# A Hyena loop that is skewed by half a channel group, its transforms copied out of PSUM by ScalarE

## The chip, the cores and the metric

The kernel runs on one core of one Trainium2 chip. TensorE (PE) multiplies matrices into PSUM, VectorE (DVE) and ScalarE (ACT) read PSUM and SBUF, GpSimd (POOL) does little here, SyncE (SP) issues the DMAs. Each engine takes its instructions in a fixed order and waits on semaphores for the others. The metric is the time of one execution in microseconds (us) on the device.

## What is computed

The reference is a two-layer diffusion backbone: an even layer with a recurrent part (RG-LRU) and a Hyena part, an odd layer with a convolution module, and after each a mixture of 16 experts. The change touches the Hyena part of the even layer alone:

```python
u = _dwconv1d(hy, p['conv_b_w'], p['conv_b_b'])     # three taps, 1536 channels
v, *gates = jnp.split(u, HYENA_ORDER + 1, axis=-1)  # 512 channels each
kf = _hyena_filters_fft(h.shape[1], p)
z = v
for o in range(HYENA_ORDER):                        # two orders, one after the other
    z = gates[o] * _fftconv(z, kf[:, o], p['filt_bias'][o])
return jnp.concatenate([y_a, z], axis=-1) @ p['w_out'], h_last
```

`_fftconv` is a convolution over 1024 tokens by a transform, a product with the filter's transform and the transform back.

## The kernel before

The 512 channels go in four groups of 128, and each group passes two convolutions, one for each order. I call the first convolution of group i J0(i) and the second J1(i); J1(i) starts from the gated result of J0(i). So there are eight jobs, and each is made of these steps:

- `short(ct)`: one projection on PE, 48 matmuls of 128x512 at lines 153 to 155 into one of two wide PSUM tiles `P`, then the three taps: ACT at line 767, DVE at lines 768 and 769. It gives a tile `y`: the input of J0, or a gate. There are twelve in the loop. The weights of a projection come in by `piece`, which splits them in two (ACT line 158, DVE line 159).
- `tok(y)`: eight transposes on PE (line 649) and two ACT copies (line 650) give `ut`, with tokens on the partitions.
- `hy_fwd`: 16 matmuls on PE (line 593) into four PSUM tiles `q`, and four ACT copies (line 596) of the second half of each.
- `hy_st1`: the radix-2 step, eight DVE operations of 128x256 (lines 603, 604), one operand in PSUM.
- `hy_mid`: two `fft8` (two operations of 128x512 and fourteen of 128x256 each, lines 565 to 582), and between them eight operations of 128x1024 (lines 614 to 621): the product with the filter's transform `K` and the first step back. All on DVE, all in SBUF.
- `hy_inv`: 16 matmuls on PE (line 632) into two PSUM tiles.
- `hy_gate`: two DVE products (line 640) of the PSUM tiles with the gate, written every eighth element into `zt`. For J0, `tok` follows, for J1 a store or the output projection.

`fill(n)` puts n pieces of other work between: four matmuls each (line 229) for the adaLN vectors, with a load of 1 MB each. `gate(ct)` is one of two more projections, for the RG-LRU output. The `K` of a job is loaded in `hy_fwd` into a ring of four buffers that the fills use too.

The program writes the jobs as J0(0), J1(0), J0(1), J1(1) and so on. A scheduler of the framework then sorts each engine's instructions, and that order is fixed when the program is built. The order of the twelve projections is 0, 4, 8, 1, 5, 9, 2, 6, 10, 3, 7, 11. Small PSUM tiles come from a pool of four, and all jobs use one pool of three SBUF tiles (tag `X`) for `pq` and `E`.

Of the kernel before, what the change touches and what calls it, by code (L numbers as in the profile page):

```python
# [9 lines left out]
F32 = mybir.dt.float32  # L10
# [5 lines left out]
OP = mybir.AluOpType  # L16
# [129 lines left out]
class Builder:  # L146
# [185 lines left out]
    def filt_mlp(self, p, f):  # L332
        nc, A = self.nc, self.A
        V = nc.vector
        zT = f.tile([66, 512], F32, name="zT")
# [42 lines left out]
    def filters(self, fk, other):  # L378
        nc, A = self.nc, self.A
        V = nc.vector  # L380
        c = math.sqrt(0.5)
# [201 lines left out]

    def hy_fwd(self, p, J):
        nc = self.nc
        J["K"] = K = self.wr.tile([128, 8, 2, 128], F32, name="w", tag="w")
        nc.sync.dma_start(K, self.kd[J["o"]][J["qd"]])
        J["q"] = []
        for a in range(4):
            q = self.ps.tile([128, 2, 2, 128], F32, name="q", tag="n")  # L590
            for j in range(2):
                for ri in range(2):
                    nc.tensor.matmul(q[:, j, ri], self.G[:, a + 4 * j, ri * 128:ri * 128 + 128], J["u"][:, a + 4 * j],  # L593
                                     start=True, stop=True)
            y4 = p.tile([128, 2, 128], F32, name="y4", tag="y4", bufs=2)
            nc.scalar.copy(y4, q[:, 1])
            J["q"].append((q, y4))

    def hy_st1(self, p, J):
        V = self.nc.vector  # L600
        J["pq"] = pq = p.tile([128, 8, 2, 128], F32, name="pq", tag="X", bufs=3)
        for a, (q, y4) in enumerate(J["q"]):
            V.tensor_tensor(pq[:, a], q[:, 0], y4, op=OP.add)
            V.tensor_tensor(pq[:, 4 + a], q[:, 0], y4, op=OP.subtract)

    def hy_mid(self, p, J):
        V = self.nc.vector
        pq, K = J["pq"], J["K"]
        E = p.tile([128, 8, 2, 128], F32, name="E", tag="X", bufs=3)
        sub = p.tile([128, 4, 2, 128], F32, name="sub", tag="sub", bufs=1)  # L610
        self.fft8(pq, E, -1, sub)
        Z = pq
        tmp = sub.rearrange("p a b c -> p (a b) c")
        V.tensor_tensor(Z[:, :, 0], E[:, :, 0], K[:, :, 0], op=OP.mult)
        V.tensor_tensor(tmp, E[:, :, 1], K[:, :, 1], op=OP.mult)
        V.tensor_tensor(Z[:, :, 0], Z[:, :, 0], tmp, op=OP.subtract)
        V.tensor_tensor(Z[:, :, 1], E[:, :, 0], K[:, :, 1], op=OP.mult)
        V.tensor_tensor(tmp, E[:, :, 1], K[:, :, 0], op=OP.mult)
        V.tensor_tensor(Z[:, :, 1], Z[:, :, 1], tmp, op=OP.add)
        V.tensor_tensor(E[:, 0:4], Z[:, 0:4], Z[:, 4:8], op=OP.add)  # L620
        V.tensor_tensor(E[:, 4:8], Z[:, 0:4], Z[:, 4:8], op=OP.subtract)
        self.fft8(E, Z, 1, sub)
        J["Z"] = Z
# [11 lines left out]
    def hy_gate(self, p, J):  # L635
        dst = p.tile([128, D], F32, name="zt", tag="zt", bufs=1)
        zv = dst.rearrange("q (p a) -> q a p", a=8)
        gv = J["gate"].rearrange("q (p a) -> q a p", a=8)
        for h, q in enumerate(J["r"]):
            self.nc.vector.tensor_tensor(zv[:, h * 4:h * 4 + 4], q, gv[:, h * 4:h * 4 + 4], op=OP.mult)  # L640
        return dst

    def to_tok(self, src, dst):
# [8 lines left out]
    def even_mixer(self, st, so):  # L652
        nc, tc, A = self.nc, self.tc, self.A
# [6 lines left out]
        with ExitStack() as s1, ExitStack() as sl:  # L660
# [66 lines left out]
            with ExitStack() as s2:  # L727
# [13 lines left out]
                w, P = xproj(0)  # L741
# [5 lines left out]
                for ct in range(4):  # L747
                    if ct:
                        w, P = xproj(ct)
# [7 lines left out]
            py = pool(s1, "py", "right")  # L757
            self.G = py.tile([128, 8, 256], F32, name="G2")
            gload = nc.sync.dma_start(self.G, A["G"].rearrange("p a r k -> p a (r k)"))
# [12 lines left out]
            def tok(y):  # L772
                ut = py.tile([128, 8, 128], F32, name="ut", tag="u", bufs=2)
                self.to_tok(y, ut)
                return ut

            pend = []

            def drain():
                J = pend.pop(0)  # L780
                self.hy_inv(py, J)
                z = self.hy_gate(py, J)
                if J["o"] == 0:
                    return tok(z)
                i = J["qd"]
                if i == 3:
                    return z
                nc.sync.dma_start(self.ycd[512 + i * 128:512 + (i + 1) * 128, :], z)

            for i in range(4):  # L790
                J0 = dict(o=0, qd=i, u=tok(short(i)))
                if i == 0:
                    with tc.issue_after(getattr(gload, "ins", gload)):
                        nc.sync.dma_start(self.IG, A["IG"])
                        self.fill(5)
                else:
                    self.fill(5)
                self.hy_fwd(py, J0)
                self.hy_st1(py, J0)
                if pend:  # L800
                    drain()
                self.hy_mid(py, J0)
                J0["gate"] = short(4 + i)
                self.fill(5)
                g1 = short(8 + i)
                pend.append(J0)
                J1 = dict(o=1, qd=i, u=drain(), gate=g1)
                self.hy_fwd(py, J1)
                self.hy_st1(py, J1)
                self.hy_mid(py, J1)  # L810
                pend.append(J1)
            for _ in range(len(self.ada_todo) + len(self.ada_have)):
                self.fill()
            for ct in (2, 3):
# [10 lines left out]
            with tc.tile_pool(name="pq0", bufs=1, reuse_waits="tile") as pq, \  # L825
                    tc.manual_schedule(engines={mybir.EngineType.PE, mybir.EngineType.DVE, mybir.EngineType.Activation}):
                y = self.y_load(pq, 0, 1)
                th = pq.tile([128, 7, 128], F32R, name="th")
                tl = pq.tile([128, 7, 128], F32R, name="tl")
                for q in range(2):  # L830
                    self.wide_hi(po, ws[q])
                    self.wide_lo(po, ws[q], q)
                self.mix_cast(0)
                self.bcast(self.sh2b, 0, 1)
                self.wide_hi(po, ws[2])
                z = drain()
                self.split(th, tl, y)
                self.split(self.zh, self.zl, z)
                self.wide_lo(po, ws[2], 2)
                self.wide_hi(po, ws[3])  # L840
                self.wide_lo(po, ws[3], 3)
                self.PP = [self.ps.tile([128, 512], F32, name="P", tag="w") for _ in range(2)]
                for k in range(8):
                    for n in range(2):
                        self.post_mm(self.PP[n], k, n, th[:, k] if k < 7 else self.zh[:, :128],
                                     tl[:, k] if k < 7 else self.zl[:, :128])
# [796 lines left out]
```

## Time and profile before

| what | value |
|---|---|
| median of three runs | 2298.85 us (2296.74 to 2299.62) |
| the profiled execution | 2297.13 us |
| its span, first to last instruction | 2295.1 us |
| PE busy over the span | 2123.7 us (93%) |
| DVE busy | 1819.8 us (79%) |
| ACT busy | 1201.7 us (52%) |
| Hyena stage, first radix-2 step to the last `fft8` | 281.45 to 547.74 us |

A PE that counts as busy is not always at its peak, since matmuls overlap in the record; what a row of equal matmuls takes from one start to the next tells its rate. The granted clock is a share of full speed: 1.0 is 2.4 GHz, 0.5 is 1.2 GHz. The rows on which the argument stands come below.

### The profile page before, as it was taken

Reading aid. Unit: us, or ns where it says so; the run is one execution under the profiler, and the core shown is the slowest. Engines: PE = TensorE matmul, PEld = TensorE weight load, DVE = VectorE, ACT = ScalarE, POOL = GpSimd, SP = SyncE. Lnnn points to the kernel's source line nnn. Section 1 sums busy time; section 2 is a strip of 40 time slices with the busy share of each in tenths; the row PEclk is TensorE's granted clock in tenths of the full one; section 3 lists DMA queues with packets and bytes.
Section 4 is the critical chain, followed back from the end, with each engine's and each line's share of the span. In section 5 each row is a group of like instructions: output and inputs, shape, how many; then the busy total and the mean of one; then the engine's idle time right before and its main releaser. Section 6 shows DMA issues by size and latency. Waiting matters only on the chain.

```text
span 2295.1 us, 29201 instructions
## 1 busy us (share of the span) xinstructions
PE 2123.7 (93%) x10882; PEld 1654.9 (72%) x10882; DVE 1819.8 (79%) x2876; ACT 1201.7 (52%) x1458; POOL 127.1 (6%) x128
## 2 busy tenths in 40 slices
PE   7999998996968999999999699979689999999997
PEld 5976766775745877877878488867457777777775
DVE  5979799998596988989888533276968898888887
ACT  3658511212214777777777521134247667676774
POOL 0000000000001000000000100010010000000001
PEclk9999999998988999999999899979789999999999
DMA  7241585564848999999998345234779999999974
GB/s 277 107 138 47 198 296 196 220 254 150 291 171 323 368 393 378 379 388 376 391 378 267 105 131 163 93 128 177 257 291 360 384 367 386 368 372 380 365 270 156
DMA packets 210023, 616.13 MB, mean 268 GB/s; under 512 B 27988, under 2 KB 76758, under 8 KB 200089
## 3 DMA queue, kind: packets, MB, share of 16 engines
q1 hardware_dynamic: 198634, 572.85, 66.3%
q0 software_dynamic: 11248, 41.42, 7.2%
q8 instruction: 85, 1.39, 0.2%
q14 instruction: 56, 0.46, 0.1%
HBM read 558.62 MB, written 55.61 MB: 268 GB/s over the span
## 4 chain that ended last, share of the span: by engine, by line
PE 77%; DVE 14%; DMA 3%; issue 3%; ACT 2%; POOL 1%; SPq 0%; POOLq 0%; ACTq 0%; DVEq 0%
PE P L153 20%; PE P L155 20%; PE P L154 19%; PE P L1251 6%; PE q L1216 2%; PE q L593 1%; PE q L229 1%; PE q L394 1%; PE q L510 1%; PE q L632 1%; PE q L1381 1%; PE q L307 1%; POOL rs L278 1%; DVE mm L873 0%; DMA xs<-h2d,ix 0%
## 5 line engine op out<-in xcount | busy, mean ns | idle before, releaser
L159 DVE TENSOR_TENSOR e<-wx,e 128x1024 fp32r<-128x1024 f32 x516 | 619.0, 1221 | 93.1 <-ACT e L158 78.5
L158 ACT CAST e<-wx 128x1024 fp32r<-128x1024 f32 x516 | 539.8, 1051 | 233.9 <-PE P L155 232.1
L153 PE MATMUL P<-e,th 128*128 128x512 f32 x1384 | 562.8, 407 | 0.2 <-ACT th L158 0.2
L155 PE MATMUL P<-e,tl 128*128 128x512 f32 x1384 | 543.5, 393 | 1.6 <-DVE tl L159 1.6
L154 PE MATMUL P<-e,th 128*128 128x512 f32 x1384 | 543.0, 392 | 0.0
L153 PEld LDWEIGHTS P<-e,th 128*128 128x128 f32 x1384 | 260.0, 188 | 61.6 <-issue 7.2
L154 PEld LDWEIGHTS P<-e,th 128*128 128x128 f32 x1384 | 260.1, 188 | 61.0 <-DVE e L159 4.3
L155 PEld LDWEIGHTS P<-e,tl 128*128 128x128 f32 x1384 | 259.7, 188 | 61.5 <-DVE tl L159 2.5
L159 DVE TENSOR_TENSOR e<-w,e 128x1024 fp32r<-128x1024 f32 x176 | 211.8, 1221 | 49.2 <-ACT e L158 29.6
L153 PE MATMUL P<-hh,wh 128*128 128x512 f32 x576 | 229.0, 399 | 7.9 <-DVE y L769 4.2
L158 ACT CAST e<-w 128x1024 fp32r<-128x1024 f32 x176 | 184.1, 1051 | 94.2 <-PE P L155 76.1
L154 PE MATMUL P<-hl,wh 128*128 128x512 f32 x576 | 228.1, 396 | 0.8 <-DVE ms L276 0.8
L155 PE MATMUL P<-hh,wlo 128*128 128x512 f32 x576 | 227.6, 395 | 0.0
L153 PEld LDWEIGHTS P<-hh,wh 128*128 128x128 f32 x576 | 108.8, 189 | 40.4 <-issue 13.2
L154 PEld LDWEIGHTS P<-hl,wh 128*128 128x128 f32 x576 | 109.0, 189 | 28.1 <-issue 5.1
L155 PEld LDWEIGHTS P<-hh,wlo 128*128 128x128 f32 x576 | 108.5, 188 | 27.0 <-issue 4.8
L1314 POOL DMA_INDIRECT acc<-yo,ix x31 | 50.6, 1634 | 934.7 <-DVE yo L1313 934.7
L159 DVE TENSOR_TENSOR tl<-q,th 128x512 fp32r<-128x512 f32 x128 | 84.6, 683 | 7.1 <-ACT th L158 5.1
L158 ACT CAST wh<-w 128x1024 fp32r<-128x1024 f32 x16 | 16.7, 1049 | 136.6 <-PE P L154 124.1
L1251 PE MATMUL P<-wx,xf 128*128 128x512 f32 x176 | 79.1, 592 | 0.0
L158 ACT CAST th<-q 128x512 fp32r<-128x512 f32 x128 | 71.7, 586 | 1.9 <-PE q L1216 1.9
L278 POOL TENSOR_TENSOR rs<-ms,nh 128x1 f32<-128x1 f32 x42 | 23.9, 570 | 830.1 <-issue 435.2
(406 smaller groups left out, 3057.8 us busy)
## 6 DMA issues: line engine op xcount, KB each, us to landing
wx<-i_exp_w SPq DMA_DIRECT2D x272, 1024.0 KB, 7.9
w<-i_exp_w SPq DMA_DIRECT2D x96, 1024.0 KB, 8.1
w<-i_w_mod SPq DMA_DIRECT2D x48, 1024.0 KB, 7.2
wst<-i_w_in SPq DMA_DIRECT2D x20, 512.0 KB, 3.9
kd<-w SPq DMA_DIRECT2D x8, 1024.0 KB, 5.0
w<-kd SPq DMA_DIRECT2D x8, 1024.0 KB
acc<-res SPq DMA_DIRECT2D x16, 512.0 KB, 3.0
e<-i_exp_w SPq DMA_DIRECT2D x16, 512.0 KB, 7.2
```

Source lines behind the costliest of these rows:

```text
L153: t.matmul(o, lh, rh, start=start, stop=False)
L154: t.matmul(o, lh, rl, start=False, stop=False)
L155: t.matmul(o, ll, rh, start=False, stop=stop)
L158: self.nc.scalar.copy(hi, src)
L159: self.nc.vector.tensor_sub(lo, src, hi.bitcast(F32))
L229: self.nc.tensor.matmul(self.ada_q[32 * j:32 * j + 32, :], self.sp[:, kc, :], w[:, j * 512:(j + 1) * 512], start=kc == 0, stop=kc == 7, ti ...
L278: nc.gpsimd.tensor_tensor(r, m, self.nh[:, :n], op=OP.pow)
L307: nc.tensor.transpose(q[:, t * 128:(t + 1) * 128], x[:, c * 128:(c + 1) * 128], self.idn)
L394: nc.tensor.matmul(q[:, j], h2[:, a + j], ws[:, o, i, cs], start=True, stop=True)
L1216: nc.tensor.transpose(q[:, j], src[:, c * 128:(c + 1) * 128], self.idn)
L1251: nc.tensor.matmul(P[:, ns], f[:, k], h[:, ns], start=k == 0, stop=k == 7)
L1314: self.last = nc.gpsimd.indirect_dma_start(self.acc[l][:, :], bass.IndirectOffsetOnAxis(ap=xT[e][1][:, 0:1], axis=0), yo, None, compute_op ...
```

## The change

Four things are written differently.

1. `hy_fwd` copies each of its four PSUM tiles whole to SBUF by ACT (128x512 in place of 128x256) into one tile `raw`.
2. The radix-2 step moves into `hy_mid` and becomes two DVE operations of 128x1024, both operands in SBUF. `raw` is then used in place of `E`. `K` is loaded here.
3. `hy_gate` has ACT copy the two PSUM tiles into `zt`, every eighth element, and then one DVE product of 128x1024 in place.
4. The loop is written with the jobs in the order J0(0), J0(1), J1(0), J0(2), J1(1), J0(3), J1(2), J1(3): the middle of J1 of a group comes half a group later. The order of the projections becomes 0, 4, 1, 8, 5, 2, 9, 6, 3, 10, 7, 11. The fills are 4, then 5 and 4 in each turn (before: 5 and 5); their number stays 40.

```diff
     def hy_fwd(self, p, J):
         nc = self.nc
-        J["K"] = K = self.wr.tile([128, 8, 2, 128], F32, name="w", tag="w")
-        nc.sync.dma_start(K, self.kd[J["o"]][J["qd"]])
-        J["q"] = []
+        J["raw"] = raw = p.tile([128, 8, 2, 128], F32, name="raw", tag="X", bufs=3)
         for a in range(4):
...
-            y4 = p.tile([128, 2, 128], F32, name="y4", tag="y4", bufs=2)
-            nc.scalar.copy(y4, q[:, 1])
-            J["q"].append((q, y4))
-
-    def hy_st1(self, p, J):
-        V = self.nc.vector
-        J["pq"] = pq = p.tile([128, 8, 2, 128], F32, name="pq", tag="X", bufs=3)
-        for a, (q, y4) in enumerate(J["q"]):
-            V.tensor_tensor(pq[:, a], q[:, 0], y4, op=OP.add)
-            V.tensor_tensor(pq[:, 4 + a], q[:, 0], y4, op=OP.subtract)
+            nc.scalar.copy(raw[:, a:a + 5:4], q)
 
     def hy_mid(self, p, J):
         V = self.nc.vector
-        pq, K = J["pq"], J["K"]
-        E = p.tile([128, 8, 2, 128], F32, name="E", tag="X", bufs=3)
+        K = self.wr.tile([128, 8, 2, 128], F32, name="w", tag="w")
+        self.nc.sync.dma_start(K, self.kd[J["o"]][J["qd"]])
+        E = J["raw"]
+        pq = p.tile([128, 8, 2, 128], F32, name="pq", tag="X", bufs=3)
+        V.tensor_tensor(pq[:, 0:4], E[:, 0:4], E[:, 4:8], op=OP.add)
+        V.tensor_tensor(pq[:, 4:8], E[:, 0:4], E[:, 4:8], op=OP.subtract)
...
     def hy_gate(self, p, J):
         dst = p.tile([128, D], F32, name="zt", tag="zt", bufs=1)
         zv = dst.rearrange("q (p a) -> q a p", a=8)
-        gv = J["gate"].rearrange("q (p a) -> q a p", a=8)
         for h, q in enumerate(J["r"]):
-            self.nc.vector.tensor_tensor(zv[:, h * 4:h * 4 + 4], q, gv[:, h * 4:h * 4 + 4], op=OP.mult)
+            self.nc.scalar.copy(zv[:, h * 4:h * 4 + 4], q)
+        self.nc.vector.tensor_tensor(dst, dst, J["gate"], op=OP.mult)
         return dst
...
+            self.hy_fwd(py, J0)
+            J1 = None
             for i in range(4):
...
                 self.hy_mid(py, J0)
                 J0["gate"] = short(4 + i)
                 self.fill(5)
+                nxt = dict(o=0, qd=i + 1, u=tok(short(i + 1))) if i < 3 else None
+                u1 = back(J0)
+                if nxt:
+                    self.hy_fwd(py, nxt)
+                if J1:
+                    self.hy_mid(py, J1)
                 g1 = short(8 + i)
...
+                self.fill(4)
+                if J1:
+                    back(J1)
+                J1 = dict(o=1, qd=i, u=u1, gate=g1)
                 self.hy_fwd(py, J1)
-                self.hy_st1(py, J1)
-                self.hy_mid(py, J1)
-                pend.append(J1)
+                J0 = nxt
+            self.hy_mid(py, J1)
```

`back(J)` is the old `drain` for a job that is given: `hy_inv`, `hy_gate`, and then `tok` or the store.

What the scheduler made of it shows at three places. In the rows, L642 is the new line of `tok`'s transposes (before L649), L625 of the inverse (before L632), L591 of the forward transform (before L593), L601 and L602 are the new radix-2 step, L632 and L633 the copy and product of the gate, L761 and L762 the taps (before L768, L769). A matmul of 128x128 in this listing is two in the trace.

The first place is PE behind the middle of J0(0); L265 belongs to the adaLN vectors and waits for DVE. Before:

```order
L265 MATMUL q<-idn,mod_138 8x128 x2
L229 MATMUL q<-w,sp 32x512 x4
L632 MATMUL q<-IG,pq 128x128 x16
L649 MATMUL q<-idn,zt 128x128 x4
L229 MATMUL q<-w,sp 32x512
L649 MATMUL q<-idn,zt 128x128 x4
L593 MATMUL q<-ut,G_2044 128x128 x16
```

Now (nine matmuls of a projection stand where the dots are):

```order
L265 MATMUL q<-idn,mod_138 8x128 x2
L642 MATMUL q<-idn,y 128x128 x8
L625 MATMUL q<-IG,pq 128x128 x16
...
L642 MATMUL q<-idn,zt 128x128 x8
L591 MATMUL q<-ut,G_2044 128x128 x16
L229 MATMUL q<-w,sp 32x512 x16
L591 MATMUL q<-ut,G_2044 128x128 x16
```

The transposes of `zt` were two groups, one for each half of the gate, and are one. The forward transform that follows them was that of J1(0); now the first is that of J0(1), whose `ut` comes from the eight transposes of `y` at the top, and that of J1(0) is the second.

The second place is DVE at the same point, from the last operations ahead of the gate. Before:

```order
L768 SCALAR_TENSOR_TENSOR y<-P,vec,y 128x1023
L159 TENSOR_TENSOR wlo<-wst,wh 128x1024
L769 SCALAR_TENSOR_TENSOR y<-P,vec,y 128x1023
L640 TENSOR_TENSOR zt<-q,y 128x4x128
L159 TENSOR_TENSOR wlo<-wst,wh 128x1024
L640 TENSOR_TENSOR zt<-q,y 128x4x128
L603 TENSOR_TENSOR pq<-q,y_2431 128x256
```

Now:

```order
L761 SCALAR_TENSOR_TENSOR y<-P,vec,y 128x1023
L159 TENSOR_TENSOR wlo<-wst,wh 128x1024
L762 SCALAR_TENSOR_TENSOR y<-P,vec,y 128x1023
L159 TENSOR_TENSOR wlo<-wst,wh 128x1024
L633 TENSOR_TENSOR zt<-zt,y 128x1024
L601 TENSOR_TENSOR pq<-raw 128x1024
L602 TENSOR_TENSOR pq<-raw 128x1024
```

The gate was two products with a split between them; it is one product behind both splits, and the middle of J0(1) stands right behind it.

The third place is PE at the end of the loop, from the last matmul of the last projection on. Before:

```order
L155 MATMUL P<-hh_151,wlo 128x512
L265 MATMUL q<-idn,gg_144 8x128
L265 MATMUL q<-idn,mod_139 8x128
L632 MATMUL q<-IG,pq 128x128 x16
L153 MATMUL P<-oh,th 128x512
```

Now:

```order
L155 MATMUL P<-hh_151,wlo 128x512
L625 MATMUL q<-IG,pq 128x128 x4
L591 MATMUL q<-ut,G_2044 128x128 x6
L625 MATMUL q<-IG,pq 128x128 x12
L591 MATMUL q<-ut,G_2044 128x128 x10
L245 MATMUL t<-idn,w 128x128 x4
L265 MATMUL q<-idn,gg_144 8x128
L265 MATMUL q<-idn,mod_139 8x128
L625 MATMUL q<-IG,pq 128x128 x16
L153 MATMUL P<-oh,th 128x512
```

Before, only the inverse of J1(3) was left behind the last projection. Now the inverse of J1(2) and the forward transform of J1(3) stand there too, with a quarter of that inverse ahead of the forward transform.

## Rows read from the trace of the kernel before

**Rows 1.** Busy time by stretch: us, PE, PEld, DVE, ACT, POOL, clock, DMA share, GB/s.

```profile
281.45:547.74 266.29, 238.73 (x1416) 171.44 (x1414) 248.21 (x440) 54.89 (x81) 0.00 (x0) 0.96 0.65 239
532.00:548.00 16.00, 1.68 (x7) 1.13 (x6) 15.74 (x23) 5.62 (x5) 0.00 (x0) 0.59 0.84 296
```

**Rows 2.** What DVE waited for, 270 to 560 us: total, times, longest.

```profile
DVE pq L603 <- ACT y L596: 17.7, 9, 7.1
DVE zt L640 <- PE q L632: 9.9, 6, 3.4
DVE y L768 <- ACT y L767: 0.9, 1, 0.9
```

**Rows 3.** DVE in order of time: start, us, line, idle before it.

```profile
281.45 0.42 DVE L603 TENSOR_TENSOR pq<-q,y 128x256 f32<-128x256 f32 x1 [7.10 <-ACT y L596]
...
310.46 0.41 DVE L582 SCALAR_TENSOR_TENSOR pq<-sub,E 128x256 f32<-128x256 f32 x1
...
547.32 0.42 DVE L582 SCALAR_TENSOR_TENSOR pq<-sub,E 128x256 f32<-128x256 f32 x1
550.76 1.10 DVE L640 TENSOR_TENSOR zt<-q,y 128x512 f32<-128x512 f32 x1 [3.02 <-PE q L632]
553.19 1.12 DVE L640 TENSOR_TENSOR zt<-q,y 128x512 f32<-128x512 f32 x1 [1.33 <-PE q L632]
```

**Rows 4.** Groups by line and shape, 260 to 560 us: busy us, mean ns, idle before.

```profile
L603 DVE TENSOR_TENSOR pq<-q,y 128x256 f32<-128x256 f32 x32 | 13.4, 418 | 18.3 <-ACT y L596 17.7
L567 DVE TENSOR_TENSOR E<-sub 128x256 f32<-128x256 f32 x8 | 3.4, 420 | 0.0
L640 DVE TENSOR_TENSOR zt<-q,y 128x512 f32<-128x512 f32 x16 | 17.9, 1128 | 10.0 <-PE q L632 9.9
L596 ACT COPY y<-q 128x256 f32<-128x256 f32 x32 | 11.9, 373 | 45.7 <-PE q L593 32.6 <-DVE pq L604 11.1 <-DVE sub L573 1.8
L650 ACT COPY ut<-q 128x512 f32<-128x512 f32 x16 | 9.1, 588 | 46.5 <-PE q L649 46.5
```

**Rows 5.** Pieces of the chain that ended last: start, us, engine, line, number.

```profile
296.66 1.13 DVE sub L615
...
304.98 0.60 DVE sub L565
...
448.06 3.66 PE q L593 x32
...
466.31 0.89 PE q L649 x8
469.94 1.85 PE q L229 x16
...
480.02 3.57 PE q L632 x32
```

**Rows 6.** PE in order of time: two matmuls of a projection, transposes between the gate's halves.

```profile
276.16 0.39 PE L153 MATMUL P<-hh,wh 128*128 128x512 f32 x1
276.39 0.39 PE L154 MATMUL P<-hl,wh 128*128 128x512 f32 x1
...
316.00 0.60 PE L649 MATMUL q<-idn,zt 128*128 128x128 f32 x4
```

**Rows 7.** ACT groups by shape, 0 to 240 us: one operation writing with a step, and without.

```profile
L330 ACT ACTIVATE h<-sx 64x512 f32<-64x512 f32 x2 | 2.2, 1117 | 2.6 <-DVE sx L327 2.6
L330 ACT ACTIVATE h<-sx 128x512 f32<-128x512 f32 x1 | 0.6, 631 | 3.7 <-DVE sx L327 3.7
```

**Rows 8.** ACT in order of time: a split's cast ahead of the taps.

```profile
419.38 1.05 ACT L158 CAST wh<-wst 128x1024 fp32r<-128x1024 f32 x1 [5.01 <-PE P L154]
420.33 1.20 ACT L767 ACTIVATE y<-P,vec 128x1024 f32<-128x1024 f32 x1
```

**Rows 9.** PE in order of time, right behind idle stretches.

```profile
365.56 0.79 PE L153 MATMUL P<-hh,wh 128*128 128x512 f32 x1 [4.17 <-DVE y L769]
...
547.79 5.36 PE L632 MATMUL q<-IG,pq 128*128 128x128 f32 x28 [3.08 <-DVE pq L582]
```

More of the change, by code (lines that the diff above doesn't have):

```diff
@@ L775, in tok, with back @@
                 return ut
-            pend = []
-            def drain():
-                J = pend.pop(0)
+            def back(J):
                 self.hy_inv(py, J)
                 z = self.hy_gate(py, J)
+                i = J["qd"]
                 if J["o"] == 0:
                     return tok(z)
-                i = J["qd"]
                 if i == 3:
@@ L788, in drain @@
                 nc.sync.dma_start(self.ycd[512 + i * 128:512 + (i + 1) * 128, :], z)
-            for i in range(4):
[L791 to L801, printed above, removed]
+            J0 = dict(o=0, qd=0, u=tok(short(0)))
+            with tc.issue_after(getattr(gload, "ins", gload)):
+                nc.sync.dma_start(self.IG, A["IG"])
+                self.fill(4)
+            self.hy_fwd(py, J0)
+            J1 = None
+            for i in range(4):
                 self.hy_mid(py, J0)
@@ L804, in even_mixer @@
                 self.fill(5)
+                nxt = dict(o=0, qd=i + 1, u=tok(short(i + 1))) if i < 3 else None
[4 more added lines that the diff above has]
+                    self.hy_mid(py, J1)
                 g1 = short(8 + i)
-                pend.append(J0)
-                J1 = dict(o=1, qd=i, u=drain(), gate=g1)
+                self.fill(4)
+                if J1:
+                    back(J1)
+                J1 = dict(o=1, qd=i, u=u1, gate=g1)
                 self.hy_fwd(py, J1)
-                self.hy_st1(py, J1)
-                self.hy_mid(py, J1)
-                pend.append(J1)
+                J0 = nxt
+            self.hy_mid(py, J1)
             for _ in range(len(self.ada_todo) + len(self.ada_have)):
@@ L835, in even_mixer @@
                 self.wide_hi(po, ws[2])
-                z = drain()
+                z = back(J1)
                 self.split(th, tl, y)
```

## The prediction, made before the changed kernel had run

> **What bounds the kernel now.** I read four views in turn. The first is the windows view of the Hyena stage [rows 1]: between the first radix-2 step and the end of the last `fft8` (547.32 + 0.42 = 547.74 [rows 3]) DVE is busy 248.21 of 266.29 us and PE 238.73. DVE sets the pace, but PE has only some 27 us of slack in 266, so work taken from DVE is soon worth nothing unless PE also comes earlier. ACT, with 54.89, is far from a bound. The second view is what DVE waits for [rows 2]: in this neighbourhood 17.7 us for the copy in `hy_fwd` (9 waits, 7.1 of it ahead of the first job) and 9.9 for the inverse (4.35 of it behind the loop: 3.02 and 1.33 [rows 3]). So 10.6 and 5.55 us of these, with 0.9 for the taps, lie within the loop, 17.05 in all; the windows view has 266.29 - 248.21 = 18.1. The third is the chain that ended last [rows 5]: through this stage it goes along DVE's middles and steps over to PE at the transforms (3.66 and 3.57 each). The fourth is PE's order of time [rows 6, 9], for how PE fills the waits of DVE.
>
> **Prices.** From start to start, DVE takes 1.13 us for 128x1024 and 0.60 for 128x512 [rows 5]; one 128x256 takes 0.33: the first `fft8` runs from 304.98 to about 310.8 [rows 3, 5], less two of 0.60, divided by fourteen. A middle without the radix-2 step is 8 x 1.13 + 4 x 0.60 + 28 x 0.33 = 20.7. On PE a projection matmul is 0.23 [rows 6], so a projection of 48 is 10.9; a fill is 1.85 / 2 = 0.93, a transposition to tokens 0.89, a forward transform 3.66, an inverse 3.57 [rows 5].
>
> **The radix-2 step.** Eight operations at 0.33 (2.7) become two at 1.13 (2.3): -0.4 for each of eight jobs, -3.3 in all. The rows show no price of PSUM as such on DVE: 418 ns with one operand in PSUM, 420 with both in SBUF [rows 4]. The Trainium skill, "Perfetto Trace Analysis", section "Optimizing Scalar/DVE Operations", puts DVE's overhead at about 60 ns on SBUF and 125 on PSUM; by it the 80 operations that leave PSUM would give 80 x 65 ns = 5.2 us more and the sum below would be +8 in place of +13. The trace doesn't bear it out in the two groups just named, so the sum goes without.
>
> **The gate.** Two strided halves of 1.10 (mean length 1128 ns [rows 3, 4], and about 1.08 from start to start) become one contiguous product of 1.13: -1.0 for each of the seven that lie ahead of the last middle, -7. What has to happen ahead of it is longer, though: ACT's copies. Each writes 128x512 with a step of eight. No row has that operation from PSUM. The bounds: 588 ns, a contiguous copy of that size from PSUM [rows 4], and 1117 ns, an ACT operation of the same length that writes with a step, where its contiguous kin takes 631 [rows 7]. I take 1.1, the row that shares the step. The copies in `hy_fwd` go from 373 to 588 ns [rows 4], 32 x 0.215 = 6.9 us on ACT, and the sixteen gate copies add 9 to 18. ACT has room, so this costs only as latency, at the places below. A copy can also stand behind other work of ACT: at 419.38 a cast of 1.05 stands in front of taps of 1.20 [rows 8]. Before, four transposes ran on PE between the gate's halves [rows 6]; now the eight wait for the whole product. On this the same section of the Trainium skill says that breaking instructions up may let work complete sooner where they cause bubbles on another engine; it speaks against the fused gate, and the trace agrees as far as that row shows PE at work between the halves.
>
> **The first start.** The first radix-2 operation needed one of four copies; now it needs all four. It began at 281.45 [rows 3] behind the first tile; three more tiles of 3.66 / 4 each, a fill between them, and a copy that is 0.2 longer make 2.7 + 0.9 + 0.2, and a further 0.3 for the fill's four matmuls being waited for: +4.15. It is bounded by 2.7 (PE runs the four without the fill) and 5.
>
> **The waits in the loop.** I went through the new order of PE, DVE and ACT with the prices above, starting at 285.6, and set each operation at the later of its engine's turn and its inputs. DVE's waits of more than 0.5 us come out at five places.
> 1. Behind the middle of J0(0). PE stands at L265 until DVE has made its input at about 311.7, then does the transposes of `y` (0.89) and the inverse (3.57); ACT copies 1.1. DVE's filler (taps and two splits) ends about 1.7 us before that. Then the gate (1.13), and behind it on PE the transposes of `zt`, and only then the forward transform of J0(1), for which DVE waits: 0.89 + 3.66 + a copy of 0.6 and what PE still has in hand = 5.7. Together 7.4. The middle of J0(1) starts at about 325.
> 2. J0(1) to J1(0). PE's order holds here, with nothing that it waits for, some 153 projection matmuls, 13 fills, three forward transforms, an inverse and four transpositions to tokens: 153 x 0.23 + 13 x 0.93 + 11.0 + 3.6 + 3.6 = 65, with the small transposes of vectors 68. DVE has two middles of 23, the gate, three pairs of taps and three splits at 1.13 each, 57. It waits for the difference, 11.1: at two projections (4.0 and 2.6) and at the gate of J0(1) (4.5).
> 3. Projections 8 and 10: 2.9 and 2.3.
> 4. Gates of J1(1) and J0(3): 3.5 and 1.65.
> 5. The end. Now the inverse of J1(2) and the forward transform of J1(3) stand behind the last projection, and PE is idle for about 9 us until the second `fft8` of J1(2) gives its first outputs. Idle stretches of 3 to 4 us were followed by slow matmuls: 0.79 in place of 0.39 for one, and 5.36 for 28 of the inverse in place of 3.57 for 32, and the stretch had a granted clock of 0.59 [rows 1, 9]. The gate of J1(2) is waited for 3.9, the radix-2 step of J1(3) 0.7, and I add 2 for the lower level of the clock.
>
> The sum of the five is 7.4 + 11.1 + 5.2 + 5.15 + 6.6 = 35.5. The 17.05 us of before go, so idle time rises by 18.4.
>
> **The end of the loop.** The last gate (two halves, 1.10 and 1.12, with waits [rows 3]) gets a copy of 1.1 on ACT for each half and then a product of 1.13: +1.2. The stages behind it wait for this product and for weights that SP loads in order; I take them as shifted by the same amount. `K` is now loaded in `hy_mid` and, by program order, later; the ring has four buffers and at one middle the load comes just in time, so I price it at nothing; if it is late, it costs up to the 5 us of rival three.
>
> **Sum.** +4.15 - 3.3 - 7.0 + 18.4 + 1.2 = +13.45; I take +13. On the profiled execution of 2297.13 us this is 2310; the median of the runs is 1.7 above that execution, so the forecast is 2312.
>
> **Rivals.** One, on the other side: DVE stays the bound and the skew does what it could, namely that forward transforms and inverses of one job run while DVE is in the middle of the other. Then the waits of rows 2 don't grow but half of their 16 us within the loop goes: +4.15 - 10.3 + 1.2 - 8 = -13, 2286; with no wait gone it is -5, 2294. For it speaks that PE is busy 238.73 of 266.29 and so has 27 us of room [rows 1]; against it that the forward transform of J0(1) stands behind the product of J0(0)'s gate on PE, and that PE has 68 us of work where DVE has 57. The point from which it decides is whether PE ends the inverse before DVE ends its filler. I put -9, 2290, and a chance of 0.18.
>
> Two: about the same. The 11.1 us of place 2 don't appear, because PE is ahead of where my walk has it by a projection (it has room for one before the first middle). That is +13.4 - 11.1 = +2.3, 2301. Chance 0.16. 0.2% of the time, 4.6 us, is about what a measurement of this kernel can tell from no change.
>
> Three: more is lost than I see: the slower clock holds from the idle stretch to the last inverse, or a `K` comes late. For it speaks that the 28 matmuls of [rows 9] lost 2.2 us; two transforms more at that rate and a wait for a load make +5, 2317. Chance 0.08.
>
> **Chances and range.** The forecast has 0.58. Faster by over 0.2%: 0.18, from rival one. Within 0.2%: 0.16. Slower: 0.58 + 0.08 = 0.66. The likeliest case alone lies between 2304 (gate copies at 0.6 save 0.5 at six gates, the first start at 2.7, half of the waits of place 2) and 2320. The range that should hold 8 in 10 reaches from 2292, into rival one, to 2322.
>
> **What would show it.** In the trace after: the first L601 at 285.6; L601 and L602 at 1.13 each; L632 at 1.1 and not 0.6; DVE's waits for the copies (L601 on ACT, L633 on ACT) and for the taps (L761 on ACT) adding up to 30 or more over the loop; the middle of J0(1) at 325, of J1(0) at 367 and of J0(2) at 399; an idle PE of some 9 us ahead of the inverse of J1(2) with a granted clock near 0.6 (part of it at the lower level, 1.2 GHz) behind it; the last `fft8` ending at 558 to 562. It is wrong if DVE's idle time in the loop is under 20 us, or if ACT's strided copies take 0.6 and the gates wait for PE alone, or if something behind 562 moves by another amount than the loop's end.

## The result and the profile after

| | before | after |
|---|---|---|
| median | 2296.74 us (2293.32 to 2299.62, five runs) | 2310.23 us (2306.26 to 2314.26, five runs) |
| ratio to before | | 1.0057, 95% interval 1.0045 to 1.0068 |
| the profiled execution, its span | 2297.13, 2295.1 us | 2312.23, 2310.5 us |
| DVE busy in the Hyena stage | 248.21 of 266.29 us | 238.99 of 273.68 us |

The change costs 13.1 us by the ratio, with an interval of 10.3 to 15.6. The forecast was 13.

The windows view of the changed kernel answers to [rows 1]: from the first radix-2 step to the end of the last `fft8`, and a stretch behind it (columns as there).

```profile
286.02:559.70 273.68, 234.22 (x1385) 171.48 (x1383) 238.99 (x385) 72.80 (x91) 0.00 (x0) 0.93 0.61 224
564.00:574.00 10.00, 7.54 (x25) 5.52 (x25) 7.60 (x5) 4.67 (x4) 0.00 (x0) 0.67 0.33 112
```

DVE has 9.2 us less to do and the stage is 7.4 us longer: its idle time rose from 18.1 to 34.7. ACT has 17.9 more, and stays far from full. In the second window, where the output projection begins, PE has a clock of 0.67.

What DVE waited for from 270 to 562 us, which answers to [rows 2] (total, times, longest):

```profile
DVE zt L633 <- ACT zt L632: 17.6, 6, 5.0
DVE pq L601 <- ACT raw L593: 16.4, 2, 10.9
DVE y L761 <- ACT y L760: 9.9, 4, 3.1
DVE pq L601 <- PE q L625: 0.8, 1, 0.8
```

The gates (L633) now wait for ACT's copies, the taps (L761) for projections that come late, and the radix-2 step (L601) for the copies of the forward transform; 10.9 of its 16.4 are the wait ahead of the first job, which stands before the stage.

Groups by line and shape, which answer to [rows 4]:

```profile
L633 DVE TENSOR_TENSOR zt<-zt,y 128x1024 f32<-128x1024 f32 x8 | 9.8, 1225 | 24.2 <-ACT zt L632 24.2
L601 DVE TENSOR_TENSOR pq<-raw 128x1024 f32<-128x1024 f32 x8 | 9.8, 1223 | 17.2 <-ACT raw L593 16.4 <-PE q L625 0.8
L593 ACT COPY raw<-q 128x512 f32<-128x512 f32 x32 | 18.8, 590 | 36.4 <-PE q L591 36.2
L632 ACT COPY zt<-q 128x512 f32<-128x512 f32 x16 | 17.3, 1113 | 47.4 <-PE q L625 46.4 <-ACT ut L643 1.0
```

The copy that writes with a step takes 1113 ns, the one without 590. DVE in order of time, the places at which it waits:

```profile
286.02 1.23 DVE L601 TENSOR_TENSOR pq<-raw 128x1024 f32<-128x1024 f32 x1 [10.92 <-ACT raw L593]
319.46 1.23 DVE L633 TENSOR_TENSOR zt<-zt,y 128x1024 f32<-128x1024 f32 x1 [2.83 <-ACT zt L632]
326.13 1.22 DVE L601 TENSOR_TENSOR pq<-raw 128x1024 f32<-128x1024 f32 x1 [5.44 <-ACT raw L593]
343.22 1.28 DVE L761 SCALAR_TENSOR_TENSOR y<-P,vec,y 128x1023 f32<-128x1023 f32 x1 [2.92 <-ACT y L760]
359.38 1.28 DVE L761 SCALAR_TENSOR_TENSOR y<-P,vec,y 128x1023 f32<-128x1023 f32 x1 [3.09 <-ACT y L760]
368.09 1.23 DVE L633 TENSOR_TENSOR zt<-zt,y 128x1024 f32<-128x1024 f32 x1 [4.97 <-ACT zt L632]
398.25 1.28 DVE L761 SCALAR_TENSOR_TENSOR y<-P,vec,y 128x1023 f32<-128x1023 f32 x1 [2.15 <-ACT y L760]
...
433.12 1.28 DVE L761 SCALAR_TENSOR_TENSOR y<-P,vec,y 128x1023 f32<-128x1023 f32 x1 [1.75 <-ACT y L760]
...
469.17 1.23 DVE L633 TENSOR_TENSOR zt<-zt,y 128x1024 f32<-128x1024 f32 x1 [2.78 <-ACT zt L632]
...
502.16 1.23 DVE L633 TENSOR_TENSOR zt<-zt,y 128x1024 f32<-128x1024 f32 x1 [1.37 <-ACT zt L632]
...
530.18 1.22 DVE L633 TENSOR_TENSOR zt<-zt,y 128x1024 f32<-128x1024 f32 x1 [4.60 <-ACT zt L632]
...
566.29 1.22 DVE L633 TENSOR_TENSOR zt<-zt,y 128x1024 f32<-128x1024 f32 x1 [6.58 <-ACT zt L632]
```

Three smaller waits (0.81, 1.03 and 0.23) are left out. All waits between the first radix-2 step and the last `fft8` add up to 34.0 us.

PE at the end of the loop, which answers to [rows 9]:

```profile
270.30 1.13 PE L642 MATMUL q<-idn,y 128*128 128x128 f32 x8 [0.99 <-ACT wh L158]
...
521.37 2.05 PE L625 MATMUL q<-IG,pq 128*128 128x128 f32 x8 [8.35 <-DVE pq L567]
...
540.30 0.37 PE L265 MATMUL q<-idn,gg 128*8 128x128 f32 x1 [8.70 <-DVE gg L259]
...
555.49 1.19 PE L625 MATMUL q<-IG,pq 128*128 128x128 f32 x4 [14.61 <-DVE pq L567]
559.76 5.39 PE L625 MATMUL q<-IG,pq 128*128 128x128 f32 x28 [3.07 <-DVE pq L582]
567.05 0.53 PE L153 MATMUL P<-oh,th 128*128 128x512 f32 x1 [1.91 <-ACT th L158]
...
569.16 0.63 PE L153 MATMUL P<-oh,th 128*128 128x512 f32 x1
...
580.38 0.39 PE L153 MATMUL P<-oh,zh 128*128 128x512 f32 x1
```

The first of these rows, the transposes of the first `y`, is the mark from which the runs below are compared, because all that stands ahead of it is the same in all kernels. PE is idle for 8.35, 8.70 and 14.61 us (before, in that stretch, for 2.02 and 11.24), and the first matmuls of the output projection take 0.63 instead of 0.39: from 567.05 to 574 us the granted clock is 0.52, near the lower of its two levels (1.2 GHz).

The 1.91 us of PE behind the last inverse are a wait for `th`, ACT's cast of results that the loop has stored earlier. It doesn't hang on the last gate: its data were loaded by about 540 us (issued at 534.20, 5.2 us to landing). But ACT takes its instructions in order, and the copies of the last gate now stand ahead of the cast. Before, and then now:

```profile
545.71 0.94 ACT L158 CAST th<-yc 128x896 fp32r<-128x896 f32 x1 [2.23 <-DMA yc<-ycd]
```

```profile
565.18 1.07 ACT L632 COPY zt<-q 128x512 f32<-128x512 f32 x1 [1.36 <-PE q L625]
566.05 0.95 ACT L158 CAST th<-yc 128x896 fp32r<-128x896 f32 x1
```

No run puts this cast ahead of the copies.

### The profile page after: what moved, and what is told of

It is laid out like the page before. It is cut to its first block, busy times and chain, and to the rows that moved or that the text cites. A ratio compares the mean times of both kernels' runs of the same rounds, so it can differ in the third digit from the quotient of the medians.

```text
span 2310.5 us, 29141 instructions
## 1 busy us (share of the span) xinstructions
PE 2129.0 (92%) x10882; PEld 1662.2 (72%) x10882; DVE 1809.9 (78%) x2820; ACT 1224.5 (53%) x1474; POOL 126.9 (5%) x128
## 4 chain that ended last, share of the span: by engine, by line
PE 78%; DVE 12%; DMA 3%; ACT 3%; issue 3%; POOL 1%; SPq 0%; POOLq 0%; ACTq 0%; DVEq 0%
PE P L153 20%; PE P L155 20%; PE P L154 20%; PE P L1243 6%; PE q L1208 2%; PE q L229 1%; PE q L625 1%; PE q L591 1%; PE q L394 1%; DMA w<-i_w_mod 1%; PE q L510 1%; PE q L1373 1%; PE q L307 1%; POOL rs L278 0%; DVE mm L865 0%
## 5 line engine op out<-in xcount | busy, mean ns | idle before, releaser
L153 PE MATMUL P<-e,th 128*128 128x512 f32 x1384 | 562.8, 407 | 0.2 <-ACT th L158 0.2
L153 PEld LDWEIGHTS P<-e,th 128*128 128x128 f32 x1384 | 260.0, 188 | 61.5 <-issue 7.2
L153 PE MATMUL P<-hh,wh 128*128 128x512 f32 x576 | 228.0, 397 | 2.3 <-DVE kT L450 1.8
L153 PEld LDWEIGHTS P<-hh,wh 128*128 128x128 f32 x576 | 108.7, 189 | 36.1 <-issue 13.5
```

The costliest lines, as they stand in the source:

```text
L153: t.matmul(o, lh, rh, start=start, stop=False)
```

## The experiments

The ledger of a run has three parts: from the mark (the first transposes of `y`) to the end of the last `fft8`, from there to the first matmul of the output projection that needs the last gate (`zh`), and from there to the end of the program. The same rows of before:

```profile
269.72 1.13 PE L649 MATMUL q<-idn,y 128*128 128x128 f32 x8 [1.72 <-DVE y L769]
...
564.57 0.39 PE L153 MATMUL P<-oh,zh 128*128 128x512 f32 x1
```

So before has 547.74 - 269.72 = 278.02 and 564.57 - 547.74 = 16.83, and 2295.1 - 269.72 = 2025.4 in all. The change has three parts that can be set apart: the radix-2 step in SBUF with ACT's copies (R), the gate with ACT's copies (G) and the order of the loop (O). All eight combinations ran. The last column is what the ratio of the timed runs gives on 2298 us, with its interval.

| parts | loop | to `zh` | all | timed runs |
|---|---|---|---|---|
| none (before) | 278.0 | 16.8 | 2025.4 | |
| R | +5.1 | +0.1 | +5.4 | +6.0 (3.2 to 8.7) |
| G | +4.5 | +3.1 | +6.0 | +6.9 (3.9 to 9.9) |
| O | +3.1 | +0.2 | +3.4 | +2.3 (-0.2 to 4.8) |
| R, G | +7.5 | +3.4 | +12.2 | +11.0 (7.8 to 14.2) |
| R, O | +8.5 | +0.0 | +8.7 | +7.8 (4.8 to 10.8) |
| G, O | +7.8 | +4.4 | +11.8 | +9.2 (6.4 to 11.9) |
| R, G, O (after) | +11.4 | +3.9 | +14.8 | +13.1 (10.3 to 15.6) |

The three middle columns come from one trace each. What is left for the stretch behind `zh`, where the instructions are the same, lies between -1.6 and +1.4 in them, and a run below shows 2.7 in the loop at unchanged instructions. So sums of these columns are good to some 3 us, and closer agreement is chance.

**R alone.** The old loop and gate, with `hy_fwd` and `hy_mid` of the changed kernel.

```diff
-            nc.scalar.copy(y4, q[:, 1])
+            nc.scalar.copy(raw[:, a:a + 5:4], q)
...
-                self.hy_st1(py, J1)
```

> The old loop and the old gate, with only the forward transform copied whole by ACT and the radix-2 step in SBUF. Theory (latency): the radix-2 step now ends 1.8 us later behind its last tile where DVE waits for it (copy 0.59 and two operations of 1.13, before 0.37 and 0.67), and the first one starts 4.6 us later as in the changed kernel; against it 3.3 us of DVE work saved. If all eight jobs wait: about +8, 2305; with half of them hidden +3, 2300. Rival (the new loop order alone costs the time, the saving on DVE is kept): -3, 2294.

2305.44 us, +6.0, between the theory's two cases. DVE's waits for the step are four in place of nine, and longer; 4.92 us more, ahead of the step of J1(3), are put down to a small operation in front of it (L247). What it waited for, and the radix-2 steps of J1(0), J1(1) and J1(2) in order of time:

```profile
DVE pq L601 <- ACT raw L593: 24.6, 4, 10.4
...
321.52 1.22 DVE L601 TENSOR_TENSOR pq<-raw 128x1024 f32<-128x1024 f32 x1 [5.21 <-ACT raw L593]
...
388.05 1.23 DVE L601 TENSOR_TENSOR pq<-raw 128x1024 f32<-128x1024 f32 x1 [5.04 <-ACT raw L593]
...
453.82 1.23 DVE L601 TENSOR_TENSOR pq<-raw 128x1024 f32<-128x1024 f32 x1 [3.92 <-ACT raw L593]
```

In the kernel before, the same step waited 17.7 [rows 2]. The small step used each tile as it came; the large one does nothing until the fourth is copied. It happens where J1 follows its own J0, so the wait is on the path. The rival, that the order alone costs, falls: here the order is the old one.

**G alone.**

```diff
-            self.nc.vector.tensor_tensor(zv[:, h * 4:h * 4 + 4], q, gv[:, h * 4:h * 4 + 4], op=OP.mult)
+            self.nc.scalar.copy(zv[:, h * 4:h * 4 + 4], q)
+        self.nc.vector.tensor_tensor(dst, dst, J["gate"], op=OP.mult)
```

> The old loop and the old radix-2 step, with only the gate as two ACT copies and one product. Theory (latency): an ACT copy of 1.1 stands behind the last inverse tile where before a DVE product of 1.1 did, and then the whole product of 1.13 in place of nothing: the four gates of J0 and the last gate of J1 end 1.2 later, three gates of J1 save 1.0 of DVE: +3, 2300. Rival (the loop order alone costs): DVE saves 1.0 at each of seven gates: -7, 2290.

2304.24 us, +6.9: more than the theory's +3, and the opposite of the rival. What DVE waited for:

```profile
DVE pq L603 <- ACT y L596: 22.4, 13, 6.8
DVE zt L640 <- ACT zt L639: 18.7, 8, 5.7
```

The gates' waits grew from 9.9 to 18.7, and the radix-2 steps behind them from 17.7 to 22.4. In the ledger 4.5 lie in the loop and 3.1 in the stretch to `zh`, where PE waits for `th` as in the changed kernel; -1.6 is left for what follows. The runs on the clock below take this up.

**O alone.** The new loop with the old `hy_gate`, `hy_st1` right behind the old `hy_fwd`, and `K` loaded in `hy_mid`.

```diff
-            nc.scalar.copy(raw[:, a:a + 5:4], q)
+            nc.scalar.copy(y4, q[:, 1])
...
+        self.hy_st1(p, J)
```

> Only the new loop order (with the loads of K in the middle), with the old forward transform, radix-2 step from PSUM and old gate. Theory (the waits that the new order makes are what outweighs the saving): DVE work as before, waits about +12 to +18: 2309 to 2315, so at least as slow as the changed kernel. Rival (the parts cost the time by their latency, the order hides transforms): -5 to 0, 2292 to 2297.

2300.96 us, an interval from -0.2 to +4.8; the trace has +3.4. Neither expectation holds: the theory's +12 to +18 is far too much, the rival's gain is not there. The order costs little by itself, if anything, and saves nothing.

**R and G, without the order.**

```diff
-            def back(J):
+            pend = []
+            def drain():
```

> The changed kernel's forward transform, radix-2 step and gate in the old loop order. The single parts lost, from the first transposes of the loop to the end of the last gate, 5.2 us (radix-2 step), 6.3 (gate) and 3.3 (order). Theory (each is a latency on the path from one job to the next, and the order neither hides nor makes much): the two parts add up, +11 to +12 against the kernel before, 2308 to 2311. Rival (the new order is what these parts need, it hides most of what they add): clearly worse than the changed kernel, 2315 or more.

2310.08 us, +11.0, within the forecast for the sum. The order isn't what these parts need.

**R and O, the old gate.**

```diff
-            self.nc.scalar.copy(zv[:, h * 4:h * 4 + 4], q)
-        self.nc.vector.tensor_tensor(dst, dst, J["gate"], op=OP.mult)
+            self.nc.vector.tensor_tensor(zv[:, h * 4:h * 4 + 4], q, gv[:, h * 4:h * 4 + 4], op=OP.mult)
```

> The changed kernel with the old gate: new order, ACT copies and radix-2 step in SBUF. From the first transposes of the loop to the end of the program the single parts lost 5.4 us (radix-2 step), 6.0 (gate) and 3.4 (order), which add up to the 14.8 of the changed kernel. Theory (the costs add up, the order neither hides nor worsens them): 5.4 + 3.4 = +8.8 against the kernel before, 2307; against the changed kernel -6. Rival (the order does hide the longer transforms, and the sum of three is chance): +4 or less, 2302.

2305.68 us; +8.7 in the trace, where 8.8 was expected.

**G and O, the old radix-2 step.**

```diff
-            nc.scalar.copy(raw[:, a:a + 5:4], q)
+            nc.scalar.copy(y4, q[:, 1])
```

> The old forward transform and radix-2 step, with the new order and the new gate; the eighth corner of the three parts. From the first transposes of the loop to the end of the program. Theory (costs add up): 3.4 (order) + 6.0 (gate) = +9.4 against the kernel before, 2308. Rival (the order hides the gate's copies behind the middle of the other job): +5 or less, 2303.

2307.88 us, +9.2; +11.8 in the trace, of which +7.8 in the loop (4.5 + 3.1 = 7.6 was the sum) and +4.4 behind it.

With the order, R costs 8.5 - 3.1 = 5.4 in the loop and 5.1 without it; G costs 4.7 and 4.5. The order hides nothing of either. R and G do share a part in the loop: with R in place G adds 7.5 - 5.1 = 2.4, and 11.4 - 8.5 = 2.9 with the order as well. That the three single parts add up in all to just the 14.8 of the changed kernel is luck in the last digit; in the loop they make 12.7 where it has 11.4.

**The four copies, in smaller steps.** R alone, with four operations of 128x512.

```diff
-        V.tensor_tensor(pq[:, 0:4], E[:, 0:4], E[:, 4:8], op=OP.add)
-        V.tensor_tensor(pq[:, 4:8], E[:, 0:4], E[:, 4:8], op=OP.subtract)
+        for a in (0, 2):
+            V.tensor_tensor(pq[:, a:a + 2], E[:, a:a + 2], E[:, a + 4:a + 6], op=OP.add)
+            V.tensor_tensor(pq[:, a + 4:a + 6], E[:, a:a + 2], E[:, a + 4:a + 6], op=OP.subtract)
```

> As the run with the radix-2 step alone, but in four operations of 128x512 in place of two of 128x1024, so that the first two need two of the four copies. Theory (that run lost by waiting for all four copies and by the 2.3 us of work behind the last): the step ends 1.1 earlier behind the last copy, 0.6 x 2 in place of 1.13 x 2, at four to five jobs that wait, and DVE's own work rises by 0.14 for a job: -4 against that run, 2301. Rival (that run lost by ACT's longer copies and the PSUM tiles they hold): no change, 2305.

2301.82 us, a ratio of 1.0017 (1.0008 to 1.0026) beside 1.0026 (1.0014 to 1.0038) of R alone: the intervals overlap, and the ledgers are equal, +5.4 in both. At J1(0):

```profile
319.89 0.69 DVE L602 TENSOR_TENSOR pq<-raw 128x512 f32<-128x512 f32 x1 [3.30 <-ACT raw L593]
...
321.64 0.69 DVE L602 TENSOR_TENSOR pq<-raw 128x512 f32<-128x512 f32 x1 [0.45 <-ACT raw L593]
...
348.74 1.14 DVE L634 TENSOR_TENSOR zt<-q,y 128x512 f32<-128x512 f32 x1 [2.63 <-PE q L626]
```

The wait there falls from 5.21 to 3.75 as expected, and DVE's next wait, for the inverse, is 2.63 where R alone had 1.80. In the trace the freed time did not last; whether the 3.6 us between the medians are real stays open. Of the rival, longer copies and the PSUM tiles that they hold, the second half is not seen: PE goes through the forward transform of J1(0) no slower with R alone than in the kernel before, where it took 4.02.

```profile
317.08 3.78 PE L591 MATMUL q<-ut,G 128*128 128x128 f32 x32
```

The first half, the longer copies (0.59 in place of 0.37), is not set apart by any run. The Trainium skill, "Perfetto Trace Analysis", section "Optimizing Scalar/DVE Operations", says that breaking instructions up may let work complete sooner where ScalarE and VectorE aren't saturated but cause bubbles on other engines. DVE is busy for 93% of the stage [rows 1], so that condition, which the prediction left out, isn't plainly met here. These rows agree for the one step; the ledger shows no gain for the loop.

**The forward transform ahead of the inverse.** The changed kernel with two lines of the loop exchanged.

```diff
-                u1 = back(J0)
                 if nxt:
                     self.hy_fwd(py, nxt)
+                u1 = back(J0)
```

> The changed kernel with the forward transform of the next J0 written ahead of the inverse of the present one. Theory: the wait of 5.4 us ahead of the radix-2 step of J0(1) goes, as PE has the forward transform behind it when DVE is free; part of it comes back in the gate of J0(0), whose inverse is 3.7 later: between -5 and 0 against the changed kernel, middle -2, 2308. Rival (DVE waits for PE's amount of work in that stretch, not for its order): no change, 2310.

2315.42 us, ratio 1.0080 (1.0063 to 1.0097): 5 us slower than the changed kernel. DVE at the first gate and, later, at the radix-2 step of J1(0):

```profile
320.34 1.23 DVE L633 TENSOR_TENSOR zt<-zt,y 128x1024 f32<-128x1024 f32 x1 [6.81 <-ACT zt L632]
...
368.20 1.23 DVE L601 TENSOR_TENSOR pq<-raw 128x1024 f32<-128x1024 f32 x1 [7.83 <-PE q L625]
```

The wait of 5.44 is gone, and the gate waits 6.81 in place of 2.83: four of it are back at once. The wait at J1(0) is one that the expectation didn't have. The step reads nothing of the inverse for which it waits. It writes a `pq`, and by the program the pool `X` of three then holds the `raw` of J1(0), the `raw` of J0(2) and the tile that the inverse of J0(1) reads until 368.17:

```profile
364.43 3.74 PE L625 MATMUL q<-IG,pq 128*128 128x128 f32 x32
```

With the inverse behind the forward transform that tile comes free later. Three such waits add up to 15.2 us here, and to 0.8 in the changed kernel. A load of `K` is late by 1.61 us in this run. A larger pool wasn't tried.

**The step of ACT's copies.** The changed kernel, with `zt` written without the step.

```diff
-        zv = dst.rearrange("q (p a) -> q a p", a=8)
+        zv = dst.rearrange("q (a p) -> q a p", a=8)
```

> The changed kernel with the ACT copies of the gate written without the step of eight elements, so zt holds the tokens in another order and the outputs that hang on it are not the reference's. Theory (the copy stands on the path to the gate): a copy of 0.59 in place of 1.11, 0.5 to 0.8 at each of seven or eight gates, -4 to -6 against the changed kernel, 2305. Rival (the gates wait for PE, the copies are hidden): no change, 2310.

2305.58 us, ratio 1.0030 (1.0018 to 1.0042), some 6 us under the changed kernel by the ratios: the copies (585 ns here) are on the path. In the ledger the loop is 3.5 shorter than in the changed kernel, the stretch to `zh` 3.3. Not all of this is the copies' length: at J0(0) the transposes and the inverse took 1.06 and 3.74 us here and 1.91 and 4.07 in the changed kernel's trace, at granted clocks of 1.00 and 0.83, which is about 1.2 of the 3.5; and the stretch to `zh` has no matmuls at the lower clock behind the inverse.

**The step of DVE's products.** The kernel before; `zt` of J0 written as PSUM has it.

```diff
-        zv = dst.rearrange("q (p a) -> q a p", a=8)
+        zv = dst.rearrange("q (p a) -> q a p" if J["o"] else "q (a p) -> q a p", a=8)
```

> The kernel before, where the two gate products of the four J0 write zt in the order in which PSUM has it, without the step, and the transposes read it so; the gate tile is still read with the step. Theory (DVE and the path from the gate to the next forward transform bound the loop, and the step that is written costs): eight products at 0.60 in place of 1.09 are -4 us, 2295. Rival (reading with the step costs as much): products stay at 1.09, 2299.

2297.97 us, ratio 1.0002 (0.9990 to 1.0013). DVE at the gate of J0(0), whose two products write without a step here and read the gate with it:

```profile
312.55 1.08 DVE L640 TENSOR_TENSOR zt<-q,y 128x512 f32<-128x512 f32 x1
...
314.68 1.06 DVE L640 TENSOR_TENSOR zt<-q,y 128x512 f32<-128x512 f32 x1
```

The rival was right: one operand read with the step is enough to make it as slow (1.09 and 1.08 before). An operation of that size without a step and with one operand in PSUM, L1028 behind the loop, takes 0.69. The Trainium skill, "SBUF — State Buffer", section "Specifications (TRN2)", has lines of 16 bytes and a penalty for each crossing to a new one; every eighth element of four bytes is a new line each time. These rows agree with it for a read; for a write ACT's copies do, with 1113 ns against 585.

**The clock at the last inverse.** The kernel before with 64 matmuls more, whose results nobody reads, ahead of that inverse; and the changed kernel with 72.

```diff
+            wq = self.ps.tile([128, 4, 128], F32, name="wq", tag="n")
+            for r in range(64):
+                nc.tensor.matmul(wq[:, r % 4], self.G[:, r % 8, :128], pend[-1]["u"][:, r % 8], start=True, stop=True)
```

> The kernel before with 64 more matmuls of the forward transform's shape, whose results nobody reads, put on PE into its idle time ahead of the last inverse (14.6 us at full clock). Theory (the last inverse runs at the lower clock because PE is idle ahead of it): the inverse's 28 matmuls take 3.1 to 3.3 us in place of 5.36, -2.1, 2296.5. Rival (the inverse is slow for another cause, such as what DVE and the DMAs do at the time, or the extra work brings the clock down elsewhere): no change or slower, 2299 to 2302.

> The changed kernel with 72 such matmuls ahead of the last inverse. Theory (beside the inverse, the output projection's first sixteen matmuls ran at the lower clock there, 0.43 us from start to start in place of 0.23, because PE idles again for the copy and the product of the last gate): -2.1 at the inverse and -1.7 behind it, -3.8 against the changed kernel, 2306. Rival (as in the other run): no change, 2310.

PE in the first of the two, then in the second:

```profile
537.75 16.08 PE L818 MATMUL wq<-ut,G 128*128 128x128 f32 x128
553.67 3.74 PE L632 MATMUL q<-IG,pq 128*128 128x128 f32 x32
```

```profile
538.22 18.89 PE L810 MATMUL wq<-ut,G 128*128 128x128 f32 x144
556.96 3.75 PE L625 MATMUL q<-IG,pq 128*128 128x128 f32 x32
562.61 0.50 PE L153 MATMUL P<-oh,th 128*128 128x512 f32 x1 [1.91 <-ACT th L158]
...
564.63 0.63 PE L153 MATMUL P<-oh,th 128*128 128x512 f32 x1
```

In both the inverse takes 3.74 or 3.75 us for 32, near the 3.57 of the full clock [rows 5], in place of 5.36 for 28. From the last `fft8` to `zh` it gives 16.83 - 15.48 = 1.3 to the kernel before and 20.68 - 17.67 = 3.0 to the changed one. The times are 2297.32, ratio 0.9991 (0.9980 to 1.0003), which can't be told from before, and 2307.44, ratio 1.0042 (1.0028 to 1.0055) against 1.0057 (1.0045 to 1.0068), two intervals that overlap. So the rows show the gain at the inverse, and the times don't settle it. The first run's trace is 2.7 longer in the loop than before, ahead of anything that was changed: at J0(0) the granted clock was 0.62 from 313 to 322 us, the inverse took 5.72 in place of 3.84, and the gate waited:

```profile
320.06 1.09 DVE L640 TENSOR_TENSOR zt<-q,y 128x512 f32<-128x512 f32 x1 [2.74 <-PE q L632]
```

In the second run the idle 1.91 us behind the inverse is still there, and the output projection still starts with matmuls of 0.63. No version here beats the kernel before by more than its interval.

## Why the prediction came out, and where it didn't

- **The sum.** +13 was forecast, +13.1 measured (10.3 to 15.6). In the trace the span grew by 15.4, and by 14.8 from the mark, so the agreement to a tenth is luck. The loop grew by 11.4 where the terms give 12.25, the stretch to `zh` by 3.9 where 1.2 was taken.
- **What DVE saves.** It was forecast at -10.3, and -9.2 of busy time was measured. The price of 1.13 to 1.15 for each 128x1024 held, and no gain from leaving PSUM appeared.
- **The waits in the loop.** They were forecast at 35.5 and measured at 34.0. Place 1: 1.7 + 5.7 against 2.83 + 5.44. Place 2: 11.1 against 2.92 + 3.09 + 4.97 = 10.98. Place 3: 2.9 and 2.3 against 2.15 and 1.75. Place 4: 3.5 and 1.65 against 2.78 and 1.37. The gate of J1(2): 3.9 against 4.60. Two small waits (0.81 and 1.03) were not foreseen, the 0.7 at J1(3) was nearly nothing, and the 2 added for the lower clock stand in no wait of the loop. Walking the new order with the prices of the old rows gave the places, and the sizes to about 1 us each. The total is closer than its parts: places 3 to 5 were 4.3 too much, and place 1 with the waits not foreseen made up for 2.9 of it.
- **The first start.** It was forecast at +4.15. Measured from the mark, the first step begins 15.72 us behind it (286.02 - 270.30) and before 11.73: +3.99. But the end of that job's middle moved by 0.5 only (41.1 to 41.6 us behind the mark), since the old step spread its operations over the same copies, with waits of 1.37 and 0.92 that were counted among the 17.05.
- **ACT's copies.** The prediction took 1.1, and 1113 ns were measured, against the lower bound of 588.
- **The end: mis-sized.** +1.2 up to the end of the last gate was right (6.57 before, 7.81 after the last `fft8`). The step that failed is that what follows is shifted by the same amount: the stretch to `zh` grew by 3.9, and the prediction had named such a difference as a sign of being wrong. It named the product and the weights, but what PE waits for there is `th`, which ACT now casts behind the gate's copies. PE's two waits ahead of `zh` make 1.91 + 0.56 where before there was one of 1.74, which is 0.7 of the 3.9; the other 3 are some fourteen matmuls of the output projection at the lower clock. The inverse itself has no share: it takes 5.39 now and 5.36 before. In the run without the step the waits are 1.51 and 0.69, the next `L153` takes 0.40, and the 3.9 are down to 0.5.
- **The cause that the text gave the waits to: wrong in part.** It walked the whole change and spoke of the new order as what makes them, with the two other parts as gains of 3.3 and 7. Neither is a gain: alone R costs 5.4 and G 6.0, while the interval of O, 3.4 in its trace, reaches below zero. The order makes waits where it stands, but the old order with R and G makes about as many (36.5 us in its loop beside 34.0), at J1's radix-2 steps and at the gates. The right sum came from walking the whole change.
- **The rivals.** One fell: the order hides none of R and G. Its argument from the 27 us of room on PE was weak: 14.3 of them lie between 532 and 548 us [rows 1], where no projection is left. Two fell: the 11 us of place 2 are there. Three came in part, not as its text had it: the clock was low behind the inverse, and no `K` was late in the changed kernel.

What stays open is why the smaller steps of the radix-2 run gained nothing in the trace and perhaps something in the times, how much of R is the longer copy and how much the wait for all four, and how much of the order's own 3.4 is the slower start of J0(1).

## What to carry to other kernels

Work taken from the busiest engine was worth nothing here, because the path from one job to the next runs through it: an operation that can start on the first of four tiles, or on half of a result, can be worth more than one large operation behind the last. Cost such a change by writing out the new order of each engine with durations from the old trace and setting each operation at the later of its turn and its inputs; then price each part alone, since a right sum can hide wrong shares. Walk on into the next stage too: what moves to another engine also delays work there that has nothing to do with the change, as `th` on ACT shows, and here the next stage then began at the lower clock.

## What the runs showed that was not expected

- DVE's product of 128x512 at the gate of J0(0) takes 1.06 to 1.09 us with one operand read by a step of eight, with or without the step in what it writes.
- The clock at the start of the output projection goes with small waits. In the changed kernel PE idles 1.91 and 0.56 us there and the matmuls take 0.63, also in the run in which the inverse just ahead had run at full clock (1.91 and 0.78). In the kernel before it idles 1.74 once, and they take 0.39; in the run without the step 1.51 and 0.69, and 0.40. So it is in all fourteen traces: the six with ACT's stepped copies at the gate wait 1.91 or more for `th`, and matmuls of 0.63 follow; the other eight have none of these there. Most of the eight have a few such matmuls later, behind `zh` (before, five at about 571 us), so part of the loss is moved and not added.
- The time ahead of the mark differs between executions of the same instructions: the mark came at 266.93 us in one kernel and at 272.60 in another, with granted clocks of 0.98 and 0.91 over the first 100 us. So a difference of a few us is better read from a mark inside the trace than from two spans, and even behind the mark one trace can be off by some 3 us.

```profile
0.00:100.00 100.00, 85.20 (x678) 73.15 (x679) 72.78 (x187) 51.26 (x76) 7.21 (x19) 0.98 0.58 209
```

```profile
0.00:100.00 100.00, 83.92 (x623) 72.95 (x624) 66.66 (x171) 49.46 (x73) 7.21 (x19) 0.91 0.58 209
```

The first is the windows view of the run with the forward transform ahead of the inverse, the second that of the kernel before with more matmuls.
